# Preparing the last product's weights: out of the differential attention, beside other stages

## The chip, the cores and the metric

The kernel runs on one core of a Trainium2 chip. The metric is the device time of one execution in microseconds (us). TensorE (PE, with its weight loads PEld), VectorE (DVE), ScalarE (ACT) and GpSimd (POOL) each take their own instructions in order; SyncE (SP) issues all transfers, also in order.

## The reference

One encoder layer over two sequences of 512 tokens with 1024 features, each with a memory of 256 rows:

```
xn = rmsnorm(x);  mn = rmsnorm(mem)
u, q, k, v, xq, g = split(xn @ w_in)
y_s5   = gated output of a bidirectional state space scan of u        # S5 branch
y_diff = rmsnorm((softmax(q0 k0) - lam * softmax(q1 k1)) @ v)         # 4 heads, two score maps each, rotary q and k
y_x    = softmax(xq mk) @ mv                                          # cross attention over mn @ w_mem_kv
merged = sum_n sigmoid(g_n) * (branch_n @ w_up[n])
x = x + merged @ w_out
gate, up = split(rmsnorm(x) @ w_ffn_in)
x = x + (silu(gate) * up) @ w_ffn_out                                 # 2816 x 1024, the last product
out = rmsnorm(x)
```

## The kernel before

Features lie on partitions and both sequences side by side in the free dimension (128 x 1024 per tile). Every float32 operand is split into a rounded high part and the rest, and a product is three matmuls (helpers `split`, whose lines are L126 to L130, and `mm3`). Both feed forward products use a scheme of seven products for a 2x2 block product, with sums and differences of weight blocks and of activations.

The stages, with their places in the profile: memory projections and norms, the S5 branch with gate products between its parts (to about 383), its gated output (`w_glu`, 384 to 406), cross attention (about 410 to 526), differential attention (526 to 822), whose queue also holds the first two branches of the merge, the rest of the merge (to 905), the output product (to about 1005), the first feed forward product (22 rounds, `KFF`, to about 1415), and the last product (to about 1650).

**The preparation.** The seven-product scheme of the last product needs, for each of 36 pieces (4 row pairs by 9 column pairs), the sums of four 128x128 blocks of `w_ffn_out`, split into high and low parts. The generator `prepare` makes them. For a piece: two loads into `raw` (L504, L505); then ACT and DVE split three blocks into `hl` (128x384) and SP stores them to DRAM in `wD` (L511); four sums on POOL (L514 to L517); and at the next call a split of the four sums (`hl`, 128x512), stored too. One call of `half_piece` does one of these two halves, so there are 72 halves. `raw` and the two `hl` tiles have one buffer each. In the last product `prepared` reads `wD` back.

**Where it is called.** In cross attention (a loop over 32 steps of 128 query rows, run with two steps of lead) each step ends with one `half_piece(last_e)`, to be issued behind that step's exponential and its scaling. In differential attention (32 steps, `score`, `turn`, `outputs`, `squares`, `normed`) each step has two such calls. Between the parts of a step, `fill(n)` draws matmuls from `queue`: gate, query, key and value products, then `merges()`.

**What sets the order.** From cross attention to the end of differential attention the matmuls are kept in program order (`PE.on`). For the other engines a scheduler orders the instructions by its own timing model when the kernel is built; `issue_after` puts one behind another. Each engine then runs its list in order.

**The passage between the attentions.** The last cross attention step copies its output to `xosb` (L649) and stores it. The first query product, `dq0`, lies in two banks of tag `mm`, of which there are two, until `rotated` has read them: DVE multiplies by the cosine (tile `t`, L672) and shuffles (L674), POOL multiplies and adds (L675, L676), ACT and DVE split the result into `rh` and `rl`. Only then is there a bank for the first key product.

In the attentions `softmax_parts` gives `nb` (L429) and the exponential `e` (L434); the differential one is combined at L772. `factor` makes `rs` for the norm (L190, L191). In the first feed forward product `quadrants` sums banks on DVE (L1018), and `act_pair` with `quad_sums` (tile `ts`, L889 to L892) loads finished activations from `aD` and prepares the first two pairs for the last product.

Of the kernel before, what the change touches and what calls it, by code (L numbers as in the profile page):

```python
# [34 lines left out]
VISITS = ((0, 0, 2), (1, 0, 3), (2, 0, 3), (3, 0, 4), (0, 2, 5), (1, 3, 6), (2, 3, 6), (3, 4, 7), (0, 5, 9), (1, 6, 9),  # L35
          (2, 6, 9), (3, 7, 9))
NPAIR = 9

NG = (7, 5, 7)
ROUND = 12582912.0  # L40
# [25 lines left out]
def encoder(ctx: ExitStack, tc: tile.TileContext, a, out):  # L66
# [13 lines left out]
    def open_tags(es, side=None, **tags):  # L80

        for tag, n in tags.items():
            pools[tag] = es.enter_context(tc.tile_pool(name=tag, bufs=n, side=side, reuse_waits="tile"))
# [297 lines left out]
        next(s5)  # L381
    next(s5, None)

    open_tags(phase, zt=2, zy=4, zs=8)
    zh = [slot("zs", dt=F32R, name=f"zh{t}") for t in range(4)]
    zl = [slot("zs", dt=F32R, name=f"zl{t}") for t in range(4)]
    zs = []
    for t in range(4):
# [9 lines left out]
        for s in range(NS):  # L398
            split(*(z_[t][:, s * L : (s + 1) * L].rearrange("p (j c) -> p j c", j=T) for z_ in (zh, zl)), yt[:, :, s, :], scale=0.5)
        zs.append(yt)  # L400
    gates(NG[2])
    with behind():

        mrs = cst.tile([P, 4], F32, name="mrs")
# [6 lines left out]
    for t in range(4):  # L411
        o = proj(a["w_glu"][t], zh, zl, 4)
        sg = slot("zt", name="sg")
        for s in range(NS):
            S.activation(out=sg[:, s * L : (s + 1) * L], in_=o[s], func=AF.Tanh, scale=0.5, bias=bh[:, t : t + 1])
        for s in range(NS):
            g_ = sg[:, s * L : (s + 1) * L].rearrange("p (j c) -> p j c", j=T)
            V.scalar_tensor_tensor(out=g_, in0=g_, scalar=1.0, in1=zs[t][:, :, s, :], op0=ALU.add, op1=ALU.mult)
        nc.sync.dma_start(bD[0, t], sg)
    phase.close()  # L420

    last_x = None
# [57 lines left out]
    xa = phase.enter_context(tc.tile_pool(name="xa", bufs=2, reuse_waits="tile"))  # L480
    xcol = phase.enter_context(tc.tile_pool(name="xcol", bufs=2, reuse_waits="tile"))


    res_ = ExitStack()
    rpp = res_.enter_context(tc.tile_pool(name="rope", bufs=1, side="right", reuse_waits="tile"))
    rope = []
    for nm in ("c", "s"):
        r_ = rpp.tile([P, L], F32, tag=f"r{nm}", name=f"r{nm}")
        nc.sync.dma_start(r_, a["rope_" + nm])
        rope.append(r_)  # L490

    pes = ExitStack()
    pq = pes.enter_context(tc.tile_pool(name="pq", bufs=1, side="right", reuse_waits="tile"))
    wD = [[drp.tile([P, 7, 2, P], F32, name=f"wD{m}_{p}") for p in range(NPAIR)] for m in range(4)]

    def prepare():
        for m, lo_, hi_ in VISITS:
            for p in range(lo_, hi_):  # L500
                raw = pq.tile([P, 4, P], F32, tag="raw", name="raw")
                f = slice(2 * p * P, (2 * p + 2) * P)
                with queued():
                    nc.sync.dma_start(raw[:, 1:3], a["w_fo"][m, :, f].rearrange("p (a n) -> p a n", n=P))  # L504
                    nc.sync.dma_start(raw[:, 0::3], a["w_fo"][m + 4, :, f].rearrange("p (a n) -> p a n", n=P))  # L505
                yield
                for j, w_ in ((4, raw[:, 1:4]), (0, raw)):
                    n = w_.shape[1]
                    hl = pq.tile([P, n, 2, P], F32R, tag=f"hl{n}", name="hl")
                    split(hl[:, :, 0], hl[:, :, 1], w_, scale=0.5)  # L510
                    nc.sync.dma_start(wD[m][p][:, j : j + n], hl.bitcast(F32))  # L511
                    if j:
                        a21, a11, a12, a22 = (raw[:, i] for i in range(4))
                        PO.tensor_tensor(out=a22, in0=a21, in1=a22, op=ALU.add)  # L514
                        PO.tensor_tensor(out=a21, in0=a11, in1=a21, op=ALU.subtract)
                        PO.tensor_tensor(out=a11, in0=a22, in1=a11, op=ALU.subtract)  # L516
                        PO.tensor_tensor(out=a12, in0=a12, in1=a11, op=ALU.subtract)  # L517
                        yield

    prep = prepare()  # L520

    def half_piece(behind_):
        with ExitStack() as es_:
            for i_ in behind_:
                es_.enter_context(tc.issue_after(i_.ins))
            return next(prep, None)

    next(prep)

# [121 lines left out]
        half_piece(last_e)  # L651
    while queue:
        fill(6)
    phase.close()


    open_tags(phase, v2=2, qk=10, pT=4)
    ap_ = phase.enter_context(tc.tile_pool(name="att", bufs=2, reuse_waits="tile"))
    acol = phase.enter_context(tc.tile_pool(name="acol", bufs=2, reuse_waits="tile"))
    mask = [(i + 8) if i < 8 else (i - 8 if i < 16 else i) for i in range(32)]  # L660


# [61 lines left out]
        yield 0  # L724

    def merges():
        assert next(prep, None) is None
        pes.close()
        res_.close()
        xp_es.close()  # L730
        open_tags(mes, side="right", mg=8, y=8)
        for m in range(KD):
            if m == 4:
                b2 = merge_in(2)
            yield from merge_units(0, b0[0], m, first=True)
        for m in range(KD):
            yield from merge_units(2, b2, m)
# [88 lines left out]
    for i in range(-1, n + 3):  # L826
        if i + 1 < n:
            score(i + 1)
        if i == 22:
            queue.insert(1, first_in())  # L830
        fill(10)
        half_piece(last_e)
        if 0 <= i < n:
            turn(i)
        if 0 < i <= n and steps[i - 1][2] % 2:
            outputs(i - 1)
        fill(10)
        half_piece(last_e)
        if 1 < i <= n + 1 and steps[i - 2][2] == 3:
            squares(i - 2)  # L840
        if i > 2 and steps[i - 3][2] == 3:
            normed(i - 3)
    while queue:
        fill(6)
    assert next(todo, None) is None
    PE.on = False
    phase.close()
# [8 lines left out]
    for m in range(KD):  # L856
        for _ in merge_units(1, b1, m, last=True):
            pass

# [54 lines left out]

    def weights4(i):

        a1, a2 = (wp.tile([P, DM], F32, tag="wf", name="wf") for _ in range(2))
        nc.sync.dma_start(a1, a["w_fg"][i])  # L920
        nc.sync.dma_start(a2, a["w_fu"][i])
        res = {}

        def sp(pool, src, sfx, *names):
            n = len(names) * H
            wh, wl = (pool.tile([P, DM], F32R, tag=t_ + sfx, name=t_, bufs=2) for t_ in ("wh", "wl"))
            split(wh[:, :n], wl[:, :n], src)
            for j, nm in enumerate(names):
                res[nm] = (wh[:, j * H : (j + 1) * H], wl[:, j * H : (j + 1) * H])

        sp(wp, a1, "", "A11", "A12")
        sp(wp, a2[:, H:], "", "A22")
        yield res
# [32 lines left out]
    ops.append(operands(2))  # L966
    ops.append(operands(3))
    ses.close()
    open_tags(ses, side="right", ts=1)
    aps = fes.enter_context(tc.tile_pool(name="ffs", bufs=1, reuse_waits="tile"))  # L970
    open_tags(fes, ts2=1)
    next(w0)


# [66 lines left out]
    for i in range(KFF):  # L1041
        w = res0
        if i > 0:
            wg = weights4(i)
            w = next(wg)
            next(wg)
            next(wg)
        if i == KFF - 1:
            acts = [act_pair(0), act_pair(1, "ts2")]
            PE.on = True  # L1050

        ps = products(i, w)
        p0 = next(ps)
        if i == 0:
            for s in range(NS):
                _, bc = rstd(accs[s], DM)
                S.copy(accs[s], bc)
        gf0, gf1, up0, up1 = quadrants(ps, p0)
        ac = ap2.tile([P, NT], F32, tag="ac", name="ac")
        for s, gf, up in ((0, gf0, up0), (1, gf1, up1)):  # L1060
            cs = slice(s * L, (s + 1) * L)
            V.tensor_tensor(out=gf, in0=gf, in1=accs[s], op=ALU.mult)
            S.activation(out=ac[:, cs], in_=gf, func=AF.Tanh, scale=0.5)
            PO.tensor_tensor(out=up, in0=up, in1=accs[s], op=ALU.mult)  # L1064
            V.scalar_tensor_tensor(out=ac[:, cs], in0=ac[:, cs], scalar=1.0, in1=gf, op0=ALU.add, op1=ALU.mult)
            V.tensor_tensor(out=ac[:, cs], in0=ac[:, cs], in1=up, op=ALU.mult)
        nc.sync.dma_start(aD[i], ac)

# [15 lines left out]
    def prepared(m, p):  # L1084
# [3 lines left out]
        for j, names in ((4, ("A11", "A12", "A22")), (0, ("S3", "S2", "S4", "S1"))):  # L1088
# [1 line left out]
            n_w += 1  # L1090
            n = len(names)
            w_ = wp.tile([P, DM], F32R, tag=tag, name="w7")[:, : n * 2 * P]
            last_w = nc.sync.dma_start(w_.bitcast(F32), wD[m][p][:, j : j + n].rearrange("p j h c -> p (j h c)"))
            for i, nm in enumerate(names):
                res[nm] = w_[:, 2 * i * P : (2 * i + 1) * P], w_[:, (2 * i + 1) * P : (2 * i + 2) * P]
        return res
# [497 lines left out]
```

## Time and profile before

| | us |
|---|---|
| median of 3 runs | 1662.56 (1662.04 to 1662.89) |
| the profiled execution | 1664.35 |
| its span, first to last instruction | 1662.6 |
| busy PE / DVE / ACT / POOL | 1602.0 / 1154.2 / 636.0 / 532.2 |
| mean granted TensorE clock | 0.986 |

A row of the trace gives the line, engine, operation and operands as output<-input by the program's names. A wait is idle time of an engine ahead of an instruction, put down to the one that ended it. Busy times of engines overlap. Line numbers are those of the kernel before.

### The profile page before, as it was taken

Reading aid. Unit: us, or ns where it says so; the run is one execution under the profiler, and the core shown is the slowest. Engines: PE = TensorE matmul, PEld = TensorE weight load, DVE = VectorE, ACT = ScalarE, POOL = GpSimd, SP = SyncE. Lnnn points to the kernel's source line nnn. Section 1 sums busy time; section 2 is a strip of 40 time slices with the busy share of each in tenths; the row PEclk is TensorE's granted clock in tenths of the full one; section 3 lists DMA queues with packets and bytes.
Section 4 is the critical chain, followed back from the end, with each engine's and each line's share of the span. In section 5 each row is a group of like instructions: output and inputs, shape, how many; then the busy total and the mean of one; then the engine's idle time right before and its main releaser. Section 6 shows DMA issues by size and latency. Waiting matters only on the chain.

```text
span 1662.6 us, 21641 instructions
## 1 busy us (share of the span) xinstructions
PE 1602.0 (96%) x7812; PEld 1319.6 (79%) x7812; DVE 1154.2 (69%) x1860; ACT 636.0 (38%) x1130; POOL 532.2 (32%) x444
## 2 busy tenths in 40 slices
PE   7999999899997999999999998999999999999997
PEld 5788788788895768867888886778888888888887
DVE  7957897145665778777546547889777777886444
ACT  5634323235553455666323334223323232331122
POOL 0001100000212544232045244555555455354242
PEclk9999999999998999999999998999999999999998
DMA  9344343736545534458454541322222222796632
GB/s 346 138 160 147 113 157 110 227 129 235 182 164 184 171 140 146 143 184 272 166 173 136 152 134 45 114 101 89 89 77 89 87 78 82 281 327 237 222 118 102
DMA packets 109354, 259.60 MB, mean 156 GB/s; under 512 B 14016, under 2 KB 42432, under 8 KB 109248
## 3 DMA queue, kind: packets, MB, share of 16 engines
q1 hardware_dynamic: 109248, 258.23, 45.6%
q8 instruction: 61, 1.00, 0.3%
q14 instruction: 45, 0.37, 0.1%
HBM read 174.85 MB, written 83.33 MB: 155 GB/s over the span
## 4 chain that ended last, share of the span: by engine, by line
PE 66%; DVE 12%; DMA 7%; issue 5%; POOL 4%; ACT 4%; SPq 1%; POOLq 0%; ACTq 0%; DVEq 0%
PE bkmm L59 58%; DMA raw<-in_w_fo 4%; PE bktr L59 3%; DVE wl L127 2%; DVE hl L130 1%; POOL up L1064 1%; ACT hl L129 1%; PE bktr L1447 1%; POOL mg L713 1%; PE bksc L59 1%; DMA yt<-bD 1%; DMA aD<-ac 1%; PE bktr L62 1%; ACT e L434 1%; POOL raw L516 1%
## 5 line engine op out<-in xcount | busy, mean ns | idle before, releaser
L59 PE MATMUL bkmm<-xh,wh 128*128 128x512 f32 x640 | 256.8, 401 | 7.9 <-DVE t L674 6.7
L59 PE MATMUL bkmm<-xh,wl 128*128 128x512 f32 x640 | 251.9, 394 | 2.6 <-DVE wl L127 2.6
L59 PE MATMUL bkmm<-xl,wh 128*128 128x512 f32 x640 | 251.8, 393 | 0.0
L59 PE MATMUL bkmm<-tl,wh 128*128 128x512 f32 (+1 forms) x621 | 242.6, 391 | 3.5 <-DVE tl L127 3.5
L59 PE MATMUL bkmm<-th,wl 128*128 128x512 f32 (+1 forms) x621 | 241.2, 390 | 3.3 <-DVE wl L127 3.3
L59 PE MATMUL bkmm<-th,wh 128*128 128x512 f32 (+1 forms) x621 | 242.9, 391 | 0.0
L126 ACT CAST wh<-wf 128x1024 fp32r<-128x1024 f32 (+1 forms) x133 | 117.7, 885 | 236.7 <-PE bkmm L59 221.8
L127 DVE TENSOR_TENSOR wl<-wf,wh 128x1024 fp32r<-128x1024 f32 (+1 forms) x133 | 141.7, 1065 | 65.5 <-ACT wh L126 59.1
L59 PEld LDWEIGHTS bkmm<-xh,wh 128*128 128x128 f32 x640 | 121.0, 189 | 39.7 <-issue 7.5
L514 POOL TENSOR_TENSOR raw<-raw 128x128 f32<-128x128 f32 x36 | 17.0, 473 | 408.0 <-DVE hl L130 340.1
L59 PEld LDWEIGHTS bkmm<-xh,wl 128*128 128x128 f32 x640 | 120.9, 189 | 30.8 <-DVE wl L127 3.8
L59 PEld LDWEIGHTS bkmm<-tl,wh 128*128 128x128 f32 x621 | 117.4, 189 | 28.8 <-DVE tl L127 4.7
L59 PEld LDWEIGHTS bkmm<-th,wl 128*128 128x128 f32 x621 | 116.6, 188 | 29.5 <-DVE wl L127 5.8
L59 PE MATMUL bkmm<-th,w 128*128 128x512 f32 x432 | 139.0, 389 | 0.0
L59 PEld LDWEIGHTS bkmm<-xl,wh 128*128 128x128 f32 x640 | 121.1, 189 | 22.4 <-issue 0.4
L59 PEld LDWEIGHTS bkmm<-th,wh 128*128 128x128 f32 x621 | 117.3, 189 | 25.0 <-ACT wh L126 1.2
L1064 POOL TENSOR_TENSOR up<-up,acc 128x512 f32<-128x512 f32 x44 | 84.6, 1942 | 125.0 <-DVE up L1018 125.0
L59 PEld LDWEIGHTS bkmm<-th,w 128*128 128x128 f32 x432 | 81.1, 188 | 17.1 <-DVE up L1018 0.3
L126 ACT CAST wh<-ws 128x1024 fp32r<-128x1024 f32 x44 | 46.1, 1051 | 102.6 <-PE bkmm L59 72.8
L59 PE MATMUL bkmm<-tl,w 128*128 128x512 f32 x216 | 84.0, 389 | 0.0
L434 ACT ACTIVATE e<-bksc,nb 128x512 f32<-128x512 f32 (+1 forms) x96 | 58.7, 614 | 46.0 <-DVE nb L429 27.4
L59 PE MATMUL bkmm<-yh,wh 128*128 128x512 f32 x192 | 75.9, 397 | 0.3 <-DVE gl L709 0.3
(628 smaller groups left out, 3535.5 us busy)
## 6 DMA issues: line engine op xcount, KB each, us to landing
wf<-in_w_in SPq DMA_DIRECT2D x40, 512.0 KB, 3.9
wD<-hl SPq DMA_DIRECT2D x36, 512.0 KB, 2.9
w<-wD SPq DMA_DIRECT2D x36, 512.0 KB, 4.7
wD<-hl SPq DMA_DIRECT2D x36, 384.0 KB, 2.3
w<-wD SPq DMA_DIRECT2D x36, 384.0 KB, 3.4
gD<-gt SPq DMA_DIRECT2D x24, 512.0 KB, 3.0
gl<-gD SPq DMA_DIRECT2D x24, 512.0 KB, 3.4
wf<-in_w_fg SPq DMA_DIRECT2D x22, 512.0 KB, 3.5
```

What stands on the lines that cost most here:

```text
L59: return self.put(self.eng.matmul(*args, **kw))
L62: return self.put(self.eng.transpose(*args, **kw))
L126: h = S.copy(hi, src)
L127: l_ = V.tensor_tensor(out=lo, in0=src, in1=hi.bitcast(F32), op=ALU.subtract)
L129: h = S.activation(out=hi, in_=src, func=AF.Copy, scale=scale)
L130: l_ = V.scalar_tensor_tensor(out=lo, in0=src, scalar=scale, in1=hi.bitcast(F32), op0=ALU.mult, op1=ALU.subtract)
L434: last_x = S.activation(out=e, in_=sc, func=AF.Exp, bias=nb, scale=scale, accum_out=sm)
L514: PO.tensor_tensor(out=a22, in0=a21, in1=a22, op=ALU.add)
L516: PO.tensor_tensor(out=a11, in0=a22, in1=a11, op=ALU.subtract)
L713: PO.tensor_tensor(out=mg[m], in0=mg[m], in1=gt, op=ALU.add)
L1064: PO.tensor_tensor(out=up, in0=up, in1=accs[s], op=ALU.mult)
L1447: PE.matmul(ps[:, g * P : (g + 1) * P], w_[:, gg * P : (gg + 1) * P], u_[:, 8 * o + gg, :], start=True, stop=True)
```

## The change

The preparation is spread over other stages. `prepare` now takes the pieces to make and a stack for its buffers, and `NPREP = (20, 28)` cuts the 36 pieces in three groups. The first 20 are called once after each of the last seven gate products, once after each of the four gated S5 outputs, and then by the calls in cross attention; the group must be done when cross attention ends, and its buffers are closed there. Differential attention has no calls. Pieces 20 to 27 start when its last step is issued: one call per `fill(24)` of what is left in the queue, and one per tile of the merge's last branch. Pieces 28 to 35 run in rounds 1 to 18 of the first feed forward product, one call per round, behind the round's last tanh and last bank sum. The tag `qk` gets 12 buffers instead of 10, the pools of the attention tiles are closed earlier, the rotary tables are loaded earlier, and the pools of `ts` and `ts2` open only when the last preparation is done.

```diff
+NPREP = (20, 28)
...
+    def prepare(es_, pieces_):
+        pq = es_.enter_context(tc.tile_pool(name="pq", bufs=1, side="right", reuse_waits="tile"))
+        for m, p in pieces_:
...
-    gates(NG[2])
+    pes = ExitStack()
+    prep = prepare(pes, pieces[: NPREP[0]])
+    next(prep)
+    for _ in range(NG[2]):
+        gates(1)
+        half_piece()
...
         nc.sync.dma_start(bD[0, t], sg)
+        half_piece()
...
         half_piece(last_e)
     while queue:
         fill(6)
+    assert next(prep, None) is None
+    pes.close()
     phase.close()
...
-    open_tags(phase, v2=2, qk=10, pT=4)
-    ap_ = phase.enter_context(tc.tile_pool(name="att", bufs=2, reuse_waits="tile"))
-    acol = phase.enter_context(tc.tile_pool(name="acol", bufs=2, reuse_waits="tile"))
+    open_tags(phase, v2=2, qk=12, pT=4)
+    aes = ExitStack()
+    ap_ = aes.enter_context(tc.tile_pool(name="att", bufs=2, reuse_waits="tile"))
+    acol = aes.enter_context(tc.tile_pool(name="acol", bufs=2, reuse_waits="tile"))
...
         fill(10)
-        half_piece(last_e)
         if 0 <= i < n:
             turn(i)
...
         fill(10)
-        half_piece(last_e)
...
+    aes.close()
+    prep = prepare(pes, pieces[NPREP[0] : NPREP[1]])
+    next(prep)
     while queue:
-        fill(6)
+        fill(24)
+        half_piece()
...
         for _ in merge_units(1, b1, m, last=True):
             pass
+        half_piece()
+    assert next(prep, None) is None
+    pes.close()
...
-    open_tags(ses, side="right", ts=1)
...
-    open_tags(fes, ts2=1)
...
+        if i == 1:
+            prep = prepare(pes, pieces[NPREP[1] :])
+            next(prep)
+        elif i == KFF - 3:
+            assert next(prep, None) is None
+            pes.close()
+            open_tags(ses, side="right", ts=1)
+            open_tags(fes, ts2=1)
...
         nc.sync.dma_start(aD[i], ac)
+        if 1 <= i < KFF - 3:
+            half_piece((last_t, last_sum))
```

More of the change, by code (lines that the diff above doesn't have):

```diff
@@ L382, in encoder, with half_piece @@
     next(s5, None)
+    res_ = ExitStack()
+    rpp = res_.enter_context(tc.tile_pool(name="rope", bufs=1, side="right", reuse_waits="tile"))
+    rope = []
+    for nm in ("c", "s"):
+        r_ = rpp.tile([P, L], F32, tag=f"r{nm}", name=f"r{nm}")
+        nc.sync.dma_start(r_, a["rope_" + nm])
+        rope.append(r_)
+    pieces = [(m, p) for m, lo_, hi_ in VISITS for p in range(lo_, hi_)]
+    wD = {mp: drp.tile([P, 7, 2, P], F32, name=f"wD{mp[0]}_{mp[1]}") for mp in pieces}
+    def prepare(es_, pieces_):
+        pq = es_.enter_context(tc.tile_pool(name="pq", bufs=1, side="right", reuse_waits="tile"))
+        for m, p in pieces_:
+            raw = pq.tile([P, 4, P], F32, tag="raw", name="raw")
+            f = slice(2 * p * P, (2 * p + 2) * P)
+            with queued():
+                nc.sync.dma_start(raw[:, 1:3], a["w_fo"][m, :, f].rearrange("p (a n) -> p a n", n=P))
+                nc.sync.dma_start(raw[:, 0::3], a["w_fo"][m + 4, :, f].rearrange("p (a n) -> p a n", n=P))
+            yield
+            for j, w_ in ((4, raw[:, 1:4]), (0, raw)):
+                n = w_.shape[1]
+                hl = pq.tile([P, n, 2, P], F32R, tag=f"hl{n}", name="hl")
+                split(hl[:, :, 0], hl[:, :, 1], w_, scale=0.5)
+                nc.sync.dma_start(wD[m, p][:, j : j + n], hl.bitcast(F32))
+                if j:
+                    a21, a11, a12, a22 = (raw[:, i] for i in range(4))
+                    PO.tensor_tensor(out=a22, in0=a21, in1=a22, op=ALU.add)
+                    PO.tensor_tensor(out=a21, in0=a11, in1=a21, op=ALU.subtract)
+                    PO.tensor_tensor(out=a11, in0=a22, in1=a11, op=ALU.subtract)
+                    PO.tensor_tensor(out=a12, in0=a12, in1=a11, op=ALU.subtract)
+                    yield
+    def half_piece(behind_=()):
+        with ExitStack() as es_:
+            for i_ in behind_:
+                es_.enter_context(tc.issue_after(i_.ins))
+            return next(prep, None)
     open_tags(phase, zt=2, zy=4, zs=8)
@@ L481, in encoder @@
     xcol = phase.enter_context(tc.tile_pool(name="xcol", bufs=2, reuse_waits="tile"))
[L484 to L528, printed above, removed]
     queue = []
@@ L726, in merges @@
     def merges():
-        assert next(prep, None) is None
-        pes.close()
         res_.close()
@@ L917, in weights4 @@
     def weights4(i):
+        nonlocal last_w
         a1, a2 = (wp.tile([P, DM], F32, tag="wf", name="wf") for _ in range(2))
         nc.sync.dma_start(a1, a["w_fg"][i])
-        nc.sync.dma_start(a2, a["w_fu"][i])
+        last_w = nc.sync.dma_start(a2, a["w_fu"][i])
         res = {}
@@ L1062, in encoder @@
             V.tensor_tensor(out=gf, in0=gf, in1=accs[s], op=ALU.mult)
-            S.activation(out=ac[:, cs], in_=gf, func=AF.Tanh, scale=0.5)
+            last_t = S.activation(out=ac[:, cs], in_=gf, func=AF.Tanh, scale=0.5)
             PO.tensor_tensor(out=up, in0=up, in1=accs[s], op=ALU.mult)
@@ L1092, in prepared @@
             w_ = wp.tile([P, DM], F32R, tag=tag, name="w7")[:, : n * 2 * P]
-            last_w = nc.sync.dma_start(w_.bitcast(F32), wD[m][p][:, j : j + n].rearrange("p j h c -> p (j h c)"))
+            last_w = nc.sync.dma_start(w_.bitcast(F32), wD[m, p][:, j : j + n].rearrange("p j h c -> p (j h c)"))
             for i, nm in enumerate(names):
```

## The prediction

> **What bounds the kernel now.** I read the page first, for the shares of the engines:
>
> ```profile
> PE 1602.0 (96%) x7812; PEld 1319.6 (79%) x7812; DVE 1154.2 (69%) x1860; ACT 636.0 (38%) x1130; POOL 532.2 (32%) x444
> ```
>
> TensorE (PE) works nearly all the time and the change takes no matmul away, so only PE's idle time and half-clock time can move. The table by stage shows where that lies (from and to in us; busy time and count of PE, weight loads, DVE, ACT, POOL; granted clock; DMA share; GB/s):
>
> ```profile
> 410.00:526.00 116.00, 112.14 (x656) 97.09 (x655) 77.32 (x221) 57.26 (x147) 24.32 (x47) 1.00 0.50 169
> 526.00:546.00 20.00, 13.31 (x45) 10.17 (x44) 8.94 (x15) 4.23 (x8) 9.61 (x14) 0.66 0.45 158
> 546.00:822.00 276.00, 264.22 (x1456) 210.04 (x1455) 205.96 (x371) 158.20 (x355) 90.34 (x116) 0.99 0.52 177
> 822.00:905.00 83.00, 82.69 (x363) 67.59 (x362) 42.90 (x53) 18.71 (x25) 38.25 (x14) 1.00 0.50 165
> 1025.00:1130.00 105.00, 102.35 (x446) 83.07 (x446) 90.81 (x98) 28.73 (x37) 60.07 (x34) 1.00 0.26 92
> ```
>
> Rows one to five are cross attention, the passage into differential attention, differential attention, the rest of the merge, and the start of the first feed forward product. In the third row PE idles 11.8 us; that is all that removing the preparation can give there. PE's waits in that stretch (for whom: us, times, longest):
>
> ```profile
> PE bktr L62 <- DVE rs L191: 5.1, 2, 2.9
> PE bkmm L59 <- DVE wl L127: 1.9, 1, 1.9
> PE bktr L62 <- DVE e L772: 1.7, 2, 1.1
> PE bksc L59 <- ACT e L434: 1.7, 2, 1.4
> PE bktr L62 <- DVE pL L127: 1.3, 1, 1.3
> ```
>
> They sum to 11.7 us. The second row holds the one large wait of the middle of the kernel. The timelines of ACT, DVE and PE show its cause (start, duration, then idle time before and who ended it):
>
> ```profile
> 526.71 0.63 ACT L129 ACTIVATE hl<-raw 128x512 fp32r<-128x512 f32 x1 [2.48 <-POOL raw L517]
> 527.57 0.59 ACT L649 COPY xosb<-bkoo 128x512 f32<-128x512 f32 x1 [0.23 <-PE bkoo L59]
> 531.75 0.52 ACT L129 ACTIVATE hl<-raw 128x384 fp32r<-128x384 f32 x1 [3.60 <-DMA raw<-in_w_fo]
> 536.20 0.63 ACT L129 ACTIVATE hl<-raw 128x512 fp32r<-128x512 f32 x1 [3.93 <-POOL raw L517]
> 537.45 0.63 ACT L129 ACTIVATE rh<-t 128x512 fp32r<-128x512 f32 x1 [0.61 <-POOL t L676]
> ```
> ```profile
> 532.31 0.56 DVE L130 SCALAR_TENSOR_TENSOR hl<-raw,hl 128x384 fp32r<-128x384 f32 x1 [4.25 <-ACT hl L129]
> 532.79 0.68 DVE L672 TENSOR_TENSOR t<-bkmm,rc 128x512 f32<-128x512 f32 x1
> 533.39 0.72 DVE L674 STREAM_SHUFFLE t<-bkmm 128x512 f32<-128x512 f32 x1
> ```
> ```profile
> 534.17 0.79 PE L59 MATMUL bkmm<-xh,wh 128*128 128x512 f32 x1 [6.69 <-DVE t L674]
> ```
>
> The preparation is a chain with one buffer per tile: load raw, ACT hl, DVE hl on three blocks (the 128x384 half), four POOL sums, ACT hl, DVE hl on four blocks (128x512), and only then the next load. ACT and DVE take their instructions in order, so a half that is not ready holds everything behind it. Here the first query product's two banks (both of tag mm) wait for DVE's rotary step t, t stands behind one hl, and PE has no bank for the first key product until the shuffle ends near 534.1.
>
> **The change, part by part.** The built programs' instruction orders show the same instructions on every engine, and PE in the same order except for a few matmuls in the gate product of the S5 branch and in the last merge. What moves are the 72 halves. Before: 23 by 526 and 49 between 526 and 788. After: 11 beside the gate products and the gated S5 output, 29 in and behind cross attention, none in differential attention, 16 in the merge, 16 in the first feed forward product.
>
> *The passage, plus 19.4 us.* The order of the changed program puts six halves on ACT between the last xosb and the first rh, where two stood; DVE has them all ahead of the first t. I number the halves: after's 12th to 34th stand where before's 1st to 24th stand, relative to softmax and transposes, so the 34th falls where before's 24th ran (526.71). Before, t followed the 25th; after, it follows the 40th, which is five more. Inside a piece the shortest step in the timeline is 478.78 - 475.42 = 3.36 us, from a piece to the next 531.75 - 526.71 = 5.04. Five more are 3 x 3.36 + 2 x 5.04 = 20.2, and the last is the longer form, plus 0.24 (0.63 + 0.69 against 0.52 + 0.56). Nothing covers them: PE's queue is in order, and its next matmul needs the bank. From this comes what the chain may be ahead: one step fewer lies in the same stretch of cross attention, so the 34th can run as early as the transposed block before it ends on ACT (523.86 + 0.37), 2.5 us sooner; I take 1.0. Upper bound: before's own steps here with rotary work between (4.45, 5.48, 4.24, 5.64) give 3 x 4.35 + 2 x 5.56 + 0.24 = 24.4. Lower: 20.4 - 2.5 = 17.9. PE's half clock after the wait (0.43 us from matmul to matmul from 534.17 to 540.1) is paid once before and once after. SP's next weight load also stands behind the last stores of hl, but PE is then as late as the load.
>
> *Differential attention, minus 9.4 us.* Each wait above, and what of it hl causes. The rs wait of 2.9 ends at 616: ACT had lost 1.70 + 1.77 us waiting for two halves and 1.16 in them, more than the wait: 2.9 back. The other (2.2) had one ACT and one DVE half in its chain: 1.0. wl: 0.5 on ACT and 0.6 on DVE, 1.1 of 1.9. e, exp and pL: one DVE half of 0.6 to 0.7 each, and some waiting on ACT: 0.9 + 1.0 + 0.8 of 4.7. Sum 7.7. After the wait for wl at 649 the clock is 0.5 for 3.4 us (652.6 to 656.0); if that wait halves, 1.7 us come back, together 9.4. Bounds: 4 (the first rs wait and the wl part alone) and 13.4 (all waits and the clock). The Trainium skill (TensorE: Matmul & The Clock Gate, What's actually happening) has the half clock follow an idle window of about 3.4 us. By it a 2.1 us wait costs no clock, and the sum would be 1.7 us higher; the granted clock here shows the drop after such a wait, so I keep 1.7.
>
> *Gates and gated output, plus 0.5 (0 to 3).* PE has no wait from 330 to 410, and mm has four banks there, each 24 matmuls of 0.224 us long, so PE is 16 us ahead of a held ACT. A half holds ACT at most one step. The first raw load shares the DMA engines with the loads of yD (281 and 310 GB/s in the 5 us slices from 320 to 330): ACT may stand some 4 us behind it, still under 16. If the cover were gone, 11 halves of 0.58 on ACT cost 6.4.
>
> *Merge, plus 0.5 (0 to 4).* One half per 5.4 us there against 4.2 per half of the chain, so it keeps up; DVE is half idle (42.90 of 83.00). But mm has two banks until the last branch, so a held gl step of DVE has only about 2 us of slack (12 matmuls of 0.224, less its 0.68). SP has the store of each hl ahead of the next w_up load, so a late hl also holds that load. One late load per piece would make the 4.
>
> *First feed forward product, minus 1.5 (-2.6 to +5).* One half each 19 us, behind the last tanh and the last bank sum, so its load has long landed. DVE is 77% busy from 1175 on and hides 0.56 to 0.69 us in the 4.3 that it has free per round; uncovered, 16 halves cost 11. Six quadrant sums (tile ts, L889 to L892), which before ran between 1049 and 1107 and blocked POOL 18.3 us for loads of aD, stand after the last half in the new order, since their pools open only then. PE waited 2.6 us for wl in that very stretch; I take 1.5 of it back. They now fill one round near 1342: 4.1 us against 4.3 free, hence the +5 end.
>
> The sum: 19.4 - 9.4 + 0.5 + 0.5 - 1.5 = 9.5 us. The profiled execution took 1664.35 (span 1662.6 and 1.75 around it), so 1673.85; that execution is 1.79 above the median 1662.56, so the median comes to 1672.1.
>
> **Rivals.** *More comes back than the waits show (faster, 0.05).* Where nothing waits, the weight loads fill 20.71 of 25 us, 82.8%; in differential attention 210.04 of 276, 76.1%. At 82.8% the stage would last 253.6, 22.4 us less, and the sum is 19.4 - 22.4 - 0.5 = -3.5: 1659.1. It decides if the gain passes 19 us. The Trainium skill (Perfetto Trace Analysis, Identifying the Most-Contended Engine) says that the busy share of weight loads, not of matmuls, tells how near PE is to its peak; by it this larger gain is there. Against it: some 0.65 us per score, before and after matmuls on 64 rows, recur in all 32 steps with no wait shown, and matmuls of 128 and 256 columns have another ratio; neither is changed.
>
> *The chain is ahead when cross attention ends (no change, 0.08).* If two of the six halves were done earlier, the passage costs about 11 and the total is 1663.7. Against it stands the order: ACT has the 34th behind the last transposed block, which PE released at 522, and one raw buffer allows no work ahead.
>
> *The moved halves disturb their new hosts (slower still, 0.12).* If merge and feed forward cost 4 and 5, and the gates 3, the sum is 19.4 - 9.4 + 12 = 22: 1684.6; with half of these extra costs 1678.3. For it: hl on DVE took from 0.54 to 1.71 us, long where POOL worked beside it, and POOL is more than half busy in the feed forward part. Against it: no PE wait there after 1130.
>
> **How the numbers follow.** My forecast has 0.75. Forecast and slower rival make "slower" 0.87, the chain ahead "same" 0.08, the larger gain "faster" 0.05; 0.2% (3.3 us) is about what a measurement of this kernel tells from no change. The range: below, passage at 17.9 and gain at 13.4 with the rest at -2.5 would give 1664.6, and I go to 1664; above, 24.4 and 4 with the rest at 0 are 1683; I stop at 1681, as both ends together are unlikely.
>
> **What would show it.** In the changed profile: no hl between about 550 and 815; six hl in a row on ACT behind the last xosb, some 8.4 us per pair; PE idle about 26 us there with DVE t as releaser; the first rs wait gone; ts near the end of the feed forward product. I am wrong if t starts before 545, or if the stage from the first key product to the last norm shrinks by over 17 us.

## The result, and the profile after

The changed kernel takes 1672.62 us (median of 4 runs, 1670.09 to 1674.34), the kernel before 1662.3 beside it (1660.98 to 1662.89). The ratio is 1.0062, with an interval of 1.0045 to 1.0079: slower, about as forecast (1672.1). The profiled execution took 1672.37 us with a span of 1670.6.

TensorE runs almost the same list of matmuls in both kernels, so the start of its k-th matmul can be set against the start of the k-th matmul before. The change of that difference from one place to the next says where time was lost or won. I call this the ledger; all places are times of the kernel before.

| stretch (us in before) | forecast | ledger |
|---|---|---|
| start to 330 | not in the sum | -2.5 |
| 382 to 410, gated S5 outputs | +0.5 | +4.6 |
| 410 to 527, cross attention | 0 | -1.3 |
| 527 to 534.17, passage | +19.4 | +20.5 |
| 534 to 822, differential attention | -9.4 | -14.8 |
| 822 to 925, rest of the merge | +0.5 | +6.65 |
| 1005 to 1120, start of first feed forward product | -1.5 | -5.1 |
| sum | +9.5 | +8.05 |

The two profiled times differ by 1672.37 - 1664.35 = 8.02. Two executions of unchanged code can differ too: e2, whose edit moved none of the instructions in question, stands at -1.1 at 330 and -0.3 to +0.2 in each later stretch, and e8, edited only behind 1040, spent 3.1 us more than before in differential attention, where its clock was half for two stretches of 3.41 us more (from 618.66 and 714.23). Everything ahead of 330 is of this kind.

The page's engine row: TensorE is busy 6 us less, VectorE 26 us more.

```profile
PE 1595.8 (96%) x7812; PEld 1315.4 (79%) x7812; DVE 1180.5 (71%) x1860; ACT 634.0 (38%) x1130; POOL 554.0 (33%) x444
```

The table by stage of the kernel after (columns as before; the stages have moved by their shifts):

```profile
410.00:526.00 116.00, 114.05 (x664) 98.57 (x662) 79.76 (x228) 58.23 (x149) 21.75 (x42) 1.00 0.51 170
526.00:566.00 40.00, 12.20 (x38) 9.22 (x39) 9.71 (x20) 5.93 (x10) 11.98 (x19) 0.57 0.35 125
566.00:846.00 280.00, 278.39 (x1536) 223.78 (x1535) 183.84 (x340) 139.81 (x317) 52.70 (x39) 1.00 0.28 94
829.00:917.00 88.00, 83.85 (x361) 67.00 (x360) 63.21 (x68) 26.09 (x38) 54.62 (x44) 1.00 0.79 247
1045.00:1150.00 105.00, 105.00 (x465) 86.98 (x464) 94.89 (x102) 32.51 (x44) 71.03 (x46) 1.00 0.38 128
```

In the third row TensorE idles 1.6 us of 280 where it idled 11.8 of 276: differential attention has almost no wait left. The fourth row is the merge, where it was busy 82.69 of 83 before; now 4.15 of 88 us are idle and the DMA share is 0.79 against 0.50. In the fifth row TensorE is never idle. The second row is the passage. Its timeline on ACT (start, duration, then idle time and who ended it):

```profile
528.42 0.58 ACT L653 COPY xosb<-bkoo 128x512 f32<-128x512 f32 x1 [0.17 <-PE bkoo L61]
532.79 0.52 ACT L131 ACTIVATE hl<-raw 128x384 fp32r<-128x384 f32 x1 [3.79 <-DMA raw<-in_w_fo]
536.12 0.63 ACT L131 ACTIVATE hl<-raw 128x512 fp32r<-128x512 f32 x1 [2.80 <-POOL raw L418]
...
552.89 0.63 ACT L131 ACTIVATE hl<-raw 128x512 fp32r<-128x512 f32 x1 [2.80 <-POOL raw L418]
558.23 0.63 ACT L131 ACTIVATE rh<-t 128x512 fp32r<-128x512 f32 x1 [4.71 <-POOL t L683]
```

Six halves stand between the last `xosb` and the first `rh`, and nothing else; a pair takes 541.16 - 532.79 = 8.37 us. On VectorE the first rotary step comes straight behind the sixth, and on TensorE the first key product behind the shuffle that follows:

```profile
553.55 0.69 DVE L132 SCALAR_TENSOR_TENSOR hl<-raw,hl 128x512 fp32r<-128x512 f32 x1 [2.88 <-ACT hl L131]
554.16 0.68 DVE L679 TENSOR_TENSOR t<-bkmm,rc 128x512 f32<-128x512 f32 x1
```
```profile
555.55 0.79 PE L61 MATMUL bkmm<-xh,wh 128*128 128x512 f32 x1 [27.21 <-DVE t L681]
```

The largest of TensorE's waits (us, times, longest), first from 526 to 846, where the rows of rs, wl, exp and pL are gone, then all of the gated outputs (380 to 410), which had no wait before, then the largest of the merge (846 to 930):

```profile
PE bkmm L61 <- DVE t L681: 27.2, 1, 27.2
PE bktr L64 <- DVE e L777: 1.2, 1, 1.2
```
```profile
PE bkmm L61 <- ACT sg L464: 2.1, 1, 2.1
PE bkmm L61 <- ACT wh L128: 1.1, 1, 1.1
PE bktr L64 <- DVE rs L193: 0.5, 1, 0.5
```
```profile
PE bkmm L61 <- DVE wl L129: 1.6, 4, 0.6
PE bkmm L61 <- DVE gl L716: 1.4, 1, 1.4
```

### The profile page after: what moved, and what is told of

It reads as the page before. It is cut to its first block, busy times and chain, and to the rows that moved or that the text cites. A ratio compares the mean times of both kernels' runs of the same rounds, so it can differ in the third digit from the quotient of the medians.

```text
span 1670.6 us, 21694 instructions
## 1 busy us (share of the span) xinstructions
PE 1595.8 (96%) x7812; PEld 1315.4 (79%) x7812; DVE 1180.5 (71%) x1860; ACT 634.0 (38%) x1130; POOL 554.0 (33%) x444
## 4 chain that ended last, share of the span: by engine, by line
PE 74%; DVE 10%; DMA 7%; ACT 3%; issue 2%; POOL 2%; SPq 1%; DVEq 0%; POOLq 0%; ACTq 0%
PE bkmm L61 63%; PE bktr L61 3%; DMA raw<-in_w_fo 3%; PE bksc L61 2%; PE bkoo L61 2%; PE bktr L64 2%; DVE wl L129 1%; DVE hl L132 1%; DMA yt<-bD 1%; PE bktr L1466 1%; ACT hl L131 1%; DVE st L1484 1%; ACT wh L128 1%; PE bktr L1437 1%; DVE tl L129 1%
## 5 line engine op out<-in xcount | busy, mean ns | idle before, releaser
L61 PE MATMUL bkmm<-xh,wh 128*128 128x512 f32 x640 | 256.8, 401 | 30.5 <-DVE t L681 27.2
L129 DVE TENSOR_TENSOR wl<-wf,wh 128x1024 fp32r<-128x1024 f32 (+1 forms) x133 | 149.2, 1122 | 42.9 <-ACT wh L128 34.6
L415 POOL TENSOR_TENSOR raw<-raw 128x128 f32<-128x128 f32 x36 | 24.2, 671 | 409.3 <-DVE hl L132 363.5
L132 DVE SCALAR_TENSOR_TENSOR hl<-raw,hl 128x384 fp32r<-128x384 f32 x72 | 76.6, 1064 | 77.3 <-ACT hl L131 76.8
L131 ACT ACTIVATE hl<-raw 128x384 fp32r<-128x384 f32 x72 | 41.3, 573 | 103.6 <-DMA raw<-in_w_fo 68.4
```

Source lines behind the costliest of these rows:

```text
L61: return self.put(self.eng.matmul(*args, **kw))
L129: l_ = V.tensor_tensor(out=lo, in0=src, in1=hi.bitcast(F32), op=ALU.subtract)
L131: h = S.activation(out=hi, in_=src, func=AF.Copy, scale=scale)
L132: l_ = V.scalar_tensor_tensor(out=lo, in0=src, scalar=scale, in1=hi.bitcast(F32), op0=ALU.mult, op1=ALU.subtract)
```

## The experiments

All were run against the kernel before, with the same method; edits are to the changed kernel unless said otherwise. "qk" is the tag of the rotated queries and keys, which the change gave 12 buffers instead of 10.

### What makes the passage long: e1, e3

e1 puts 17 pieces before differential attention instead of 20, and 11 into the feed forward rounds, two halves in four of them.

```diff
-NPREP = (20, 28)
+NPREP = (17, 25)
...
+            if i % 4 == 2 and i < 18:
+                half_piece((last_t, last_sum))
```

> The first group has 17 pieces instead of 20, the second still 8, the third 11 (four rounds of the first feed forward product make two halves). In the built order the 34th half is then the last one ahead of the first rotary step t. Theory A (the passage costs what the halves left over at the end of cross attention take, one step of the chain after the other): t starts behind the 34th half, near 529, PE's wait of 27.2 us shrinks to 2 or 3, and the time falls by about 25 us to 1647; the feed forward product gives back at most 3. Rival B (PE waits there for something else, the query product's banks or the key weights, and the halves only fill the time): PE restarts at 550 or later and the time stays at 1670 to 1673.

Measured: 1654.14 us (1651.48 to 1658.35), ratio 0.9954 (0.994 to 0.9969). The six halves are gone from the passage, and TensorE restarts after 2.3 us:

```profile
531.79 0.79 PE L61 MATMUL bkmm<-xh,wh 128*128 128x512 f32 x1 [2.27 <-DVE t L681]
```

The ledger of the passage is -4.7 against before, where after has +20.5. So the row of halves ahead of the first rotary step was the passage's cost, as the prediction has it. The total missed the expected 1647 above all because the end of the first feed forward product lost 8.1 us, where 3 at most were expected: the last half ran at 1365, the sums `ts` behind it at 1372 to 1380, and TensorE waited there (1360 to 1440) for weights:

```profile
PE bkmm L61 <- DVE wl L129: 6.0, 2, 4.3
```

e3 changes one number and leaves all halves where they were called:

```diff
-    open_tags(phase, v2=2, qk=12, pT=4)
+    open_tags(phase, v2=2, qk=10, pT=4)
```

> The changed kernel with 10 buffers of tag qk instead of 12; nothing else. In the built order two halves stand ahead of the first rh, and the other four lie between the following rh steps, as before. With 12 buffers the attention's e tiles come to lie in the memory that raw and hl leave; with 10 they do not. Theory A (the passage costs by how many of the 20 pieces are left over when cross attention ends): as with 12, 1670 to 1673. Theory C (the two added buffers push the next stage's tiles into the preparation's memory, and that alone brings all six halves ahead of t): t starts behind the 35th half, PE restarts near 535 to 537, and the time falls by about 20 us, to 1652 to 1655.

Measured: 1653.01 us (1652.36 to 1654.03), ratio 0.995 (0.9936 to 0.9965). The passage's ledger is +0.3, and differential attention keeps its gain (-15.8 from 534 to 790). So the calls alone do not put six halves in a row; it takes the two extra buffers with them. In the built programs, the attention's tiles `e` and `nb` lie with 12 buffers at addresses (148480 to 156864 and on) that `raw` and `hl` (149504 to 158720) still hold, and with 10 they do not. That the buffer count decides is shown. That this overlap is why the scheduler finished all halves first is inferred from the addresses, and no run shows it alone.

### The gated outputs: e5

e5 is e3 without the four calls there; their halves fall to cross attention's calls.

```diff
         nc.sync.dma_start(bD[0, t], sg)
-        half_piece()
```

> The kernel of e3 (qk with 10 buffers) without the four calls after the gated S5 outputs; its four halves fall to the calls of cross attention, and the group's last four then lie behind the first rotated tiles instead of ahead of them. Theory D, the halves that stand between the gated outputs cost the 4.6 to 6.9 us that this stage lost in after and e3: the same matmuls of 382 to 410 come within 1 us of before's, the four halves cost about 1.2 in differential attention (0.3 each, from 14.8 us for 49), and the total is e3's 1653.0 - 6.9 + 0.5 + 1.2 = 1647.8. Rival: the stage loses time to the transfers that the preparation started beside the gate products (DMA share 0.93 to 0.96 there), and the total stays at 1653 to 1654.

Measured: 1646.26 us (1646.03 to 1650.03), ratio 0.9908 (0.9885 to 0.9931), as theory D said. The table of 382 to 410 in after, and then in e5:

```profile
382.00:410.00 28.00, 24.26 (x107) 19.03 (x106) 14.16 (x20) 19.96 (x33) 4.22 (x4) 1.00 0.93 322
```
```profile
382.00:410.00 28.00, 28.00 (x127) 23.19 (x126) 16.66 (x30) 17.76 (x25) 0.00 (x0) 1.00 0.76 253
```

The ledger is 0.00 where after has +4.6 and e3 +6.9. With the halves the DMA share is 0.93, a store of `sg` lands in 6.0 us (5.6 in e5, 4.9 in before), and ACT waits up to 4.5 us for such a store before it can write `sg` again. That is only the later part of the loss, 2.4 us at 405. The first 2.1 us (385 to 391) come ahead of any store of `sg`: SP issues the loads of the memory tiles `tk` from 376.3 on instead of 372.1 (e5), behind a piece's load, so ACT squares them later (to 388.4 against 383.0), and TensorE waits for ACT's `wh` and for the norm's `rs` behind that. The preparation's transfers beside the gate products were not the cause: they are still there in e5.

### The merge: e4, e6, e7

e4 takes the 16 halves out of the merge and puts them into the feed forward rounds 1 to 14, two in each.

```diff
-NPREP = (20, 28)
+NPREP = (20, 20)
...
+            if i <= 14:
+                half_piece((last_t, last_sum))
```

> The changed kernel with the eight pieces of the second group moved to the first feed forward product: no half runs beside the merge, 32 halves run in 18 rounds (two in each of the first 14). Theory A (the 16 halves beside the merge hold DVE and POOL, and PE lost 6.6 us there): the merge between 822 and 925 gets back 6 us; the feed forward product, with DVE busy 88% in the changed kernel, goes to about 93% and loses 0 to 5: 1666 to 1671. Rival B (the merge lost by its transfers, gate tiles behind the preparation's loads and stores on SP, and would do so in the feed forward product too): the merge gets its 6 us back and the feed forward product loses as much, 1672 to 1678.

Measured: 1691.35 us (1688.96 to 1694.81), ratio 1.0186 (1.0164 to 1.0208). The merge's loss is gone (-0.1 from 822 to 925), so its halves made it. But the feed forward product lost 17.1 us from 1120 to 1402 and 5.3 behind that, where 0 to 5 were expected. One half per round is hidden there, two are not. TensorE waits (1120 to 1440) for weights that VectorE prepares:

```profile
PE bkmm L61 <- DVE wl L129: 14.2, 25, 4.3
```

VectorE's step of a half, of the kind that took 0.56 to 0.69 us in the passage, is long here in after (first row, 1120 to 1400; minimum, median and maximum in ns) and in e4 (second row):

```profile
L132 DVE SCALAR_TENSOR_TENSOR hl<-raw,hl x13: 1635/1774/1779, 1122.9 to 1348.7; 128x512 fp32r<-128x512 f32 x7, 128x384 fp32r<-128x384 f32 x6
```
```profile
L132 DVE SCALAR_TENSOR_TENSOR hl<-raw,hl x26: 691/1641/1774, 1119.7 to 1399.0; 128x384 fp32r<-128x384 f32 x13, 128x512 fp32r<-128x512 f32 x13
```

e6 makes the merge's pieces but does not store them (the last product reads eight other pieces in their place). e7 loads and stores them but splits only the first piece and leaves out the sums on POOL.

```diff
-                nc.sync.dma_start(wD[m, p][:, j : j + n], hl.bitcast(F32))
+                if (m, p) not in pieces[NPREP[0] : NPREP[1]]:
+                    nc.sync.dma_start(wD[m, p][:, j : j + n], hl.bitcast(F32))
```
```diff
+                if not only or n not in kept:
+                    hl = kept[n] = pq.tile([P, n, 2, P], F32R, tag=f"hl{n}", name="hl")
+                    split(hl[:, :, 0], hl[:, :, 1], w_, scale=0.5)
+                hl = kept[n]
...
+                if j and only:
+                    yield
+                elif j:
```

> After, where the eight pieces of the merge are made but not stored, and the last product reads eight other pieces in their place (their values are wrong; the count of loads is the same). The merge's matmuls lost 6.65 us in after, with the DMA share up from 0.50 to 0.79. Theory E, transfers: the stores (512 and 384 KB, 7.2 MB in all) delay the loads of gl, wf and yt; without them at most 2 us of the 6.65 remain and the total is 1667 to 1668. Rival F, engines in order: gl steps on DVE, weights on ACT and POOL's sums stand behind halves that wait for raw; then 4.5 us or more remain and the total is 1670 to 1672.

> After, where the merge's eight pieces are loaded and stored, but only the first is split; the other stores send the same tiles again, and the four sums of each piece on POOL are left out (their values are wrong). Theory E, transfers: the same bytes move, so 4.5 us or more of the 6.65 remain in the merge, total 1670 to 1672. Rival F, engines in order: nothing stands on ACT, DVE or POOL for the halves, at most 2 us remain, total 1667 to 1668. If e6 and e7 both keep half, it is the two together.

Measured: e6 1676.06 us (1675.43 to 1676.25), e7 1670.56 us (1669.26 to 1670.73). The ledger from 822 to 925 is +10.9 in e6 and +4.8 in e7, with +6.65 in after. Neither theory holds alone, and e6 lies above both of its ranges. Without stores the engines' order costs even more, and TensorE waits for the gate multiplication on VectorE (829 to 933; the longest wait of VectorE's own hl step there is 3.7 us, for ACT's):

```profile
PE bkmm L61 <- DVE gl L717: 5.8, 6, 2.0
```

With the transfers alone, ACT stands up to 9.8 us behind a weight load (same stretch):

```profile
ACT wh L128 <- DMA wf<-in_w_up: 17.6, 3, 9.8
```

Work in order and transfers each cost by themselves, and the two do not add. Both edits also let the scheduler place the rest anew (in e7 the stores come in bunches), so the numbers say that each is enough, not what share each has in after.

### The feed forward gain: e2, e8

Both are edits to the kernel before. e2 only opens the pools of `ts` and `ts2` late; e8 issues them behind round 18, which moved VectorE's six sums and not POOL's two.

```diff
+        if i == KFF - 3:
+            open_tags(ses, side="right", ts=1)
+            open_tags(fes, ts2=1)
```
```diff
-            acts = [act_pair(0), act_pair(1, "ts2")]
+            with tc.issue_after(hold.ins):
+                acts = [act_pair(0), act_pair(1, "ts2")]
...
+        if i == KFF - 4:
+            hold = last_sum
```

> The kernel before, with one edit: the pools of ts and ts2 open in round 19 of the first feed forward product, as in the change. Theory A (the six early quadrant sums, with POOL waiting for loads of aD, caused PE's waits for wl at the start of that product): PE has no wait for wl between 1025 and 1130, and the time falls by 4 us, to 1658. Rival B (the gain of 4.2 us that the changed kernel shows there has to do with where its other work went): the waits for wl stay at 2.6 us and the time at 1662.

> Before, with the six sums for the last product's first two pairs (tile ts, 1047 to 1107 in before) issued behind round 18 of the first feed forward product, where e2 had not moved them; nothing else. The changed kernel gained 4.2 us on the matmuls of 1050 to 1120. Theory G, these sums held POOL and DVE there: the same 3 to 4.2 us come back, total 1657.5 to 1658.5, with some of it lost again near the stage's end if they crowd there (e1 lost 8 us so, with halves beside them). Rival: the gain is due to the weights' loads or the layout of the new pools; then nothing moves, 1661 to 1663.

e2 measured 1662.1 us (1658.59 to 1663.97), ratio 1.0 (0.999 to 1.0011): its sums still ran at 1047 to 1105, so it says nothing on the theory. e8 measured 1659.92 us (1657.3 to 1667.02), ratio 0.9992 (0.9979 to 1.0005), no clear change in total. Its ledger (its profiled execution was the slowest of ten, 1667.02) bears the theory out, gain and loss: -5.0 from 1005 to 1120, in the same three steps as after (-0.87, -1.43, -2.73), and +2.8 at 1402 to 1424, where VectorE's sums (1375 to 1385) are late. So the gain in this stage comes from the sums' new place, not from the preparation. And it comes from VectorE's: POOL's two still ran at 1066 and 1102 in e8, with waits of 2.9 and 4.7 us ahead of them, while VectorE lost its 6.0 us of waits for the loads of these sums. It is free only if they end early enough: those of after began at 1353 and cost nothing.

### A better place: e9, e10, e11, e12

All are built on e5. e9 takes the halves out of the merge and calls them in differential attention, 8 feed forward pieces as before; e10 gives the feed forward rounds nine pieces.

```diff
-NPREP = (20, 28)
+NPREP = (28, 28)
...
+        if 0 <= i < 6 or 13 <= i < 21:
+            half_piece(last_e)
```

> A version put together from the runs: e5 (qk 10, no calls in the gated outputs), and the merge's 16 halves go into differential attention instead, one per step in steps 0 to 5 and 13 to 20, where two per step had cost before least (the stretches from 534 to 605 and 660 to 710 in before's time); the first feed forward product keeps its 16. By the ledgers of e5 the merge gives back 4.3 (850 to 925) and 0.8 (790 to 822). If halves at one per step cost 0.1 to 0.3 there, 14 cost 1.4 to 4.2 and the total is 1646.3 - 5.1 + 2.8 = 1644 (1642.6 to 1645.4). Rival: a step of differential attention has no room at all, and the waits for rs and wl of before come back (up to 15.8): 1647 or more.

> As e9, with 27 pieces up to differential attention (steps 0 to 5 and 15 to 20) and nine in the first feed forward product, all 18 rounds from 1 to 18. If a half per round is hidden there to the end, two halves fewer in differential attention are worth 0.2 to 0.6: 1643.5. Rival: the sums (tile ts) stand behind the last half and come too late, as in e1, where the last half was at 1365 and the stage's end lost 8.1 us; with the last half one round later than in after, the end of the stage loses 3 to 8: 1647 to 1652.

e9: 1648.5 us (1644.46 to 1648.94), ratio 0.9902 (0.9882 to 0.9922), not better than e5. Against e5 the merge gave back 5.3 us (772 to 912 in e5's time), but 4.8 us were lost in one place, 608 to 649, where the wait for rs of 2.9 us is back; from 649 to 740, with eight halves, the cost was 0.4 us. e10: 1653.61 us (1650.09 to 1654.14), ratio 0.9933 (0.9909 to 0.9956). The end of its feed forward product lost 4.4 us, with the first sums at 1367: the rival was right about the place, and its range of 1647 to 1652 was passed.

e11 moves e9's halves to steps 11 to 24. e12 also stops the calls of cross attention at its step 20 and makes two per step from 13 on.

```diff
-        if 0 <= i < 6 or 13 <= i < 21:
+        if 11 <= i < 25:
```
```diff
+        if i < 21:
             half_piece(last_e)
...
+        if 11 <= i < 25:
+            half_piece(last_e)
+            if i >= 13:
+                half_piece(last_e)
```

> As e9, with the 14 halves one per step in steps 11 to 24 instead of 0 to 5 and 13 to 20. In e9's profile, against e5's, all of the cost fell between 608 and 649 (4.8 us, the wait for rs of 2.9 us and the half clock after it), where ACT still worked off the calls of steps 0 to 5, and none between 649 and 740. If it is the backlog before the first norms, that cost goes: e9's 1648.5 - 4.8 = 1643.7 (1642.5 to 1645), rs wait gone. Rival: any halves in differential attention bring the rs wait back, at a later norm: 1647 to 1649.

> As e11, but cross attention calls a half only up to its step 20, so that none stands between the last xosb and the first rh, and the 26 left go into steps 11 and 12 (one each) and 13 to 24 (two each). The wait for t at the passage (6.4 us in e9) falls to 2 or less, as in e1 (2.3, its passage 4.7 us shorter than before's). Against it: two per step cost 2.4 + 1.4 us from 660 to 740 in before. Total e11's 1643.7 - 4.7 + 3.0 = 1642 (1639 to 1644). Rival: the two per step also bring back the waits of 740 to 780 (3.7 us): 1645 or more.

e11: 1643.02 us (1642.48 to 1646.16), ratio 0.9886 (0.9864 to 0.9907). This beats both kernels, by 1.1% and 1.8%. Its page, and its table for differential attention and the merge:

```profile
PE 1592.2 (97%) x7812; PEld 1316.0 (80%) x7812; DVE 1173.5 (72%) x1860; ACT 633.2 (39%) x1130; POOL 551.9 (34%) x444
```
```profile
546.00:790.00 244.00, 240.82 (x1361) 192.01 (x1360) 182.47 (x336) 139.89 (x317) 63.36 (x70) 1.00 0.41 137
829.00:917.00 88.00, 87.53 (x385) 71.64 (x384) 50.34 (x57) 26.75 (x33) 36.17 (x15) 1.00 0.49 156
```

In differential attention 3.2 of 244 us are idle with 14 halves called there, and the merge is back to 0.5 idle of 88. The rs wait is gone, so it was the backlog in front of the first norms, not halves as such.

e12: 1651.18 us (1650.78 to 1652.6), ratio 0.993 (0.9913 to 0.9947). Two per step lost 3.6 us from 649 to 740 and 6.5 at 740 to 762 (places in e5's time). And the passage did not shorten, though no half stands ahead of the first rotary step any more. VectorE's row there names another releaser:

```profile
526.82 0.69 DVE L677 TENSOR_TENSOR t<-bkmm,rc 128x512 f32<-128x512 f32 x1 [4.51 <-DMA bD<-xosb]
```

With 10 buffers of qk, the tile `t` lies at 136192 to 138240, across the last `xosb` (135168 to 137216), and must wait until that is stored. From the end of the copy into `xosb` to the start of `t` it took 5.1 us in e3, 4.0 in e5, 5.1 in e11, 4.2 in e12, and 4.6 in before; with 12 buffers in e1 it took 0.2. So the overlap costs about 4 us at the passage: 4.2 in e12 against 0.2 in e1, both without a half ahead of `t`. In the kernel before it and a half end almost together, so neither alone gives the time back. A version of e11 with `t` elsewhere was not tried.

## Why the prediction was right, step by step

**The passage** was sized well: +19.4 against +20.5, by six halves in a row on ACT and `t` behind them. The count and the spacing (8.37 us a pair against 3.36 + 5.04) came out of before's timeline. What it left out is one level deeper. It took the order as given and did not ask what in the diff made it: not the calls alone, but `qk=12` with them (e3). And it read before's own 6.7 us as a wait for a half only. The store of `xosb`, issued there at 529.76 and landed 2.7 us later, ended only 0.3 us before `t` started (532.79), so taking the half away gives next to nothing as long as `t` lies on `xosb`, as in e12.

**Differential attention** was undersized, -9.4 against -14.8 (-15.8 and -16.3 in e3 and e4 to 790), beyond the bound of 13.4 that the waits and the clock gave. The place was right: -3.1 at 612 to 620, where the first rs wait had been, -3.6 at 648 to 660 with the clock (the wait for wl there was 1.9 us by its row, not 2.1). What failed was the share of each wait laid to hl: I counted only the half in its own chain, while nearly all of 11.7 us went, and e9 shows why. A backlog of early halves brought the rs wait back steps later. The listed waits fell from 11.7 to 1.2 us, which is 10.5 of the 14.8, and the clock is 1.7; the other 2.6 stand in no row, and their cause stays open. The rival by the weight loads' share (22.4 us) is refuted in size: from 566 to 822 in after it is 204.58 of 256, 79.9%, with 1.2 us idle. The Trainium skill (Perfetto Trace Analysis, Identifying the Most-Contended Engine) judges headroom by that share and not by matmul time. Here TensorE's idle time and the clock, 11.8 and 1.7 us, came nearer to the gain than the share did, and 82.8% was not this stage's ceiling.

**Gates and gated output** was mis-sized: +0.5 against +4.6, beyond its bound of 3. The cover that I named, four banks of 16 us, held in the gate products (ledger 0.0 from 330 to 382) and not in the gated outputs, where ACT comes late, first by the loads of `tk` and then by the stores of `sg`. I had looked at the queue of banks, not at how soon tiles arrive and come free at a DMA share of 0.75.

**Merge** was mis-sized: +0.5 against +6.65, beyond its bound of 4. The idle VectorE that I put forward did not help, because gl stands in order behind hl steps that themselves wait (e6), and the transfers do their own harm (e7). The longest hl step on VectorE there took 2.9 us.

**First feed forward product**: -1.5 against -5.1, beyond the bound of -2.6, which had counted only the waits shown. The reason, the sums' move, is shown (e8), but it was VectorE that they held up, not POOL: of the 18.3 us that I laid to POOL, 12.9 fell at 1424, behind this stretch. That a half per round is hidden held, though the step took 1.77 us, not 0.56 to 0.69; e4, e1 and e10 show how little is left beyond that.

The errors were +1.1 (passage), +4.1 (gated outputs) and +6.15 (merge) one way, -5.4 (differential attention), -3.6 (feed forward) and -3.8 (drift to 330, and cross attention) the other. They add to -1.45: the sum was close because they cancelled, which is luck. Only the passage lay within its own bounds; it was by far the largest term that made the kernel slower, and its mechanism was right. The signs named under what would show it came out: no hl step begun between 553.6 and 826.7, six in a row, 27.2 us idle with `t` as releaser, the rs wait gone, `ts` from 1353.

## What to carry to other kernels

Work that is off the critical path has a price where an in-order engine has to run it ahead of something urgent, or where its transfers hold up an urgent load or store, so ask of each new place not how idle the engines are but which urgent instruction will stand behind it, and what it waits for itself. A changed buffer count or a moved pool can cost more than the moved work, because it decides which tiles share memory, and with that the order; compare addresses as well as instruction orders. Set the start of the same matmul in both traces against each other: a total that agrees can hide terms that are off by five microseconds each way.

## What the runs showed of the hardware

TensorE's granted clock changed only on a grid of 3.41 us, in every trace here. Around the passage it was half from 526.49 to 540.14 in before, 527.52 to 561.66 in after, 530.67 to 537.50 in e1 and 525.79 to 532.62 in e11: 4, 10, 2 and 2 steps. So behind waits of 6.7, 27.2, 2.3 and 7.1 us the half clock lasted 6.0, 6.1, 5.7 and 3.8 us from the first matmul on, which is the rest of the step that this matmul fell into and one whole step.

Whether a short wait costs clock depends on its place on that grid as well as on its length. In before, the wait of 1.9 us at 649 left 1.5 us of matmul time in its step (649.37 to 652.78), and the next step ran at half clock. The rs wait of 2.9 us was cut by a grid line at 615.24, left 1.7 us in its first step, and cost none. Over all fourteen traces, every step with less than 1.58 us of matmul time was followed by the half clock when it ran at the full one, and none with more than 2.39; between these both occur. The Trainium skill (TensorE: Matmul & The Clock Gate, What's actually happening) has the half clock after an idle window of about 3.4 us, the full one after a busy window of as much, and windows that run freely. The trace agrees on the 3.41 us, but a window counted as idle here with 1.5 us of matmuls in it.

The same hl step on VectorE took 0.56 to 0.69 us with POOL idle and 1.64 to 1.78 us in the feed forward product, where POOL is busy 172.71 of 270 us. The Trainium skill (SBUF — State Buffer, SBUF: two separate sides) says that the two engines share a pair of ports; the trace agrees, with about 1.1 us more for each such step in that product.
